# An encoder layer on one core: scores of two attention steps in one run, and feed-forward seams whose preparation is done piece by piece

## The chip, the cores and the metric

The kernel runs on one core of one Trainium2 chip. The metric is device time in microseconds (us) of one execution. PE is TensorE (matmuls), DVE is VectorE, ACT is ScalarE, POOL is GpSimd, and SP is SyncE, which here only issues DMAs. Matmul operands lie in SBUF, matmul results in PSUM, which has eight banks of 128 x 512 fp32.

## The reference

With one layer (DEPTH is 1) only the neighbourhood attention and the feed-forward are left. The same weights serve a prompt of 1024 tokens and a sample of 512 tokens, each of width 1024.

```python
h = rms_norm(x, norm_mix)
qkv = h @ w_qkv                          # 16 heads of 64
s = q . k * 64**-0.5 + bias              # each query sees a window of 8 rows x 16 columns of a grid 64 wide
o = softmax(s) @ v
x = x + o @ w_o
h = rms_norm(x, norm_ffn)
x = x + (silu(h @ w_gate) * (h @ w_up)) @ w_down      # D_FF = 2816
y = rms_norm(x, norm_final)
```

Everything is fp32.

## The kernel before

**Arithmetic.** Each fp32 operand of a matmul is split in two fp32r tiles: a "hi" copy rounded by ACT (line 138) and a "lo" rest subtracted by DVE (line 139). A product is the sum of three matmuls (hi hi, hi lo, lo hi), which is PASS. Both halves of the feed-forward use one level of a Strassen-like scheme with 7 products of 2 x 2 blocks in place of 8, so sums of blocks of the weights and of the activations must be made first, by DVE or POOL.

**Stages.** The stages follow one another on PE:

1. Norm, transposes, the V projection (lines 129, 278), then the Q and K projection of the first head pair (line 332).
2. Attention. There are 8 head pairs. A step is one column block j of a group of 512 queries and both heads of a pair: 64 steps for the prompt, 32 for the sample. A step has score matmuls `pss` (line 394), the softmax on DVE and ACT (lines 402 to 411), transposes `ptt` on PE (line 420), their split into `pT` (lines 423, 424) and the product with V, `po` (line 431). `step()` is a software pipeline: PE gets the scores of this step, the transposes of the step before, filler matmuls of the next head pair's projection (`pg`, line 332, two pieces of six), and then `po` of the step before. In the sample's steps the output projection `pgo` (line 586) is a second filler.
3. The rest of the output projection. Between its tiles, `pair()` makes the second norm of six tokens' tiles (chunk 0, the first 768 tokens), transposes them (line 668), and makes and splits the seven operands `h0` to `h6`; it does the same for chunk 1, but writes these operands to DRAM (`hop_d`, line 687). The order is: pairs of chunk 0 beside `pgo`, then the three pairs of chunk 1.
4. The feed-forward's first part: per chunk 11 units, per unit a gate and an up product (`blocks`, 7 blocks of 12 matmuls of 128 x 384, line 754). `w_ops` loads two tiles of the weight (`wr`), makes sums `wt` on DVE (lines 741 to 746) and splits into `wa` (128 x 512, six buffers) and `ws` (128 x 1024, three buffers). After chunk 0 the seven operands of chunk 1 are loaded from DRAM (`hr`) and split into the same `h` tiles. Products of a unit go to DRAM as sums (`gs`, POOL, lines 800 to 803; `gop_d`, line 805).
5. The down projection: 7 operands by 6 tiles of tokens. For each operand eleven weight tiles `wd` are split, three of the operands from differences made by POOL in `tk` (lines 848, 851, 854) and one in `dr` (line 857); for each tile one `go` (128 x 1408) is loaded and split; then 33 matmuls of 128 x 512 run (line 910). `finish()` makes the final norm and stores.

I call the borders between stages 3 and 4, between the chunks of stage 4, and between stages 4 and 5 the first, middle and third seam.

**What sets the order.** The code is written in program order for each engine, and a scheduler then orders each engine's queue by its own estimates. Every queue is executed in order, so an instruction that waits holds back all behind it on that engine. Waits come from tiles (a pool gives a tile again once its last reader is done) and from PSUM banks. PSUM tags G, S, V and T have two banks each: scores in S, transposes in T, `po` in V, projections in G.

Of the kernel before, what the change touches and what calls it, by code (L numbers as in the profile page):

```python
# [11 lines left out]
F32 = mybir.dt.float32  # L12
# [43 lines left out]
def body(tc, xp, xs, g_mix, g_ffn, g_fin, w_qkv, rpb, w_o, w_g, w_u, w_d, yp, ys):  # L56
# [9 lines left out]
    with es:  # L66
# [16 lines left out]
        hop_d = dr.tile([7, P, KB // 2, HT], F32, name="hop_d")  # L83
        gop_d = dr.tile([7, 6, P, NP, P], F32, name="gop_d")


        ident = cpool.tile([P, P + 24], F32, name="ident")[:, :P]
# [4 lines left out]
        nc.gpsimd.memset(mhalf, -0.5)  # L92

# [13 lines left out]
        def psum(tag, name, bufs=None):  # L107
            return ps.tile([P, 512], F32, tag=tag, name=name, bufs=bufs)
# [15 lines left out]
        def transpose_split(xn, hh, hl, col):  # L124
            for b in range(2):
                pt = psum("T", "pt")
# [69 lines left out]
        b_cm, bpool = pool("bpool", bufs=4)  # L196
# [33 lines left out]
        def fill_bias():  # L230
            while len(ahead) < 3:
# [183 lines left out]
        def flip(ss, n):  # L415
            out = []
            for s in ss:
                pt = psum("T", "ptt")
                for c in range(n):
                    nc.tensor.transpose(pt[:, c * P:(c + 1) * P], s[:, c * P:(c + 1) * P], ident)  # L420
                pT = ap.tile([P, 3, 2, P], F32R, tag="pT", name="pT", bufs=3)
# [25 lines left out]
        def steps(hp, g, q, k, v, n, store):  # L447
            oT = ap.tile([P, 512], F32, tag="o", name="oT", bufs=2)
            ov = oT.rearrange("p (r j i) -> p j r i", r=8, j=NJ)
            b = None  # L450
            for jj in range(2):
                pos = []
                for u in range(2):
                    j = jj * 2 + u
# [21 lines left out]
        def step(st, fillers, n):  # L476
            sc = st["s"]() if st else None
            if sc:
                next(sc)
            pT = None  # L480
# [476 lines left out]
```

## Time and profile before

| what | value |
|---|---|
| three runs | 1841.29 to 1848.37 us, median 1846.19 us |
| the profiled execution, its own time | 1845.18 us |
| its span, first to last instruction | 1843.4 us |
| PE busy | 1754.1 us, 95% of the span |
| DVE, ACT, POOL busy | 65%, 47%, 24% of the span |
| mean granted clock of PE | 0.985 |
| DMA | 278.80 MB, mean 151 GB/s |

The span and the execution's own time differ by 1.8 us, which lie around the span. "Busy" for PE includes time in which a matmul runs at a lower clock, so idle time alone does not tell what a stage loses; the count of matmuls in a stretch against its length does.

### The profile page before, as it was taken

The numbers are of one execution on the slowest core, as the hardware profiler recorded it, in microseconds if no ns is written. First come the engines' busy times: TensorE is split into PE (matmuls) and PEld (weight loads), VectorE is DVE, ScalarE is ACT, GpSimd is POOL, SyncE is SP. The second block draws the span as 40 slices with busy tenths as digits, with TensorE's granted clock in tenths as the row PEclk, the third lists the DMA queues.
The fourth block names the chain that finished last, engine by engine and source line by source line (L and its number), as shares of the span: only waits on it lengthen the run. The fifth ranks groups of instructions, "written<-read, shape, count | busy, mean of one in ns | idle before, by whom it ended". The sixth has DMA issues, their size and how long they took to land.

```text
span 1843.4 us, 25648 instructions
## 1 busy us (share of the span) xinstructions
PE 1754.1 (95%) x9178; PEld 1522.5 (83%) x9178; DVE 1192.9 (65%) x2191; ACT 863.7 (47%) x1706; POOL 448.4 (24%) x495
## 2 busy tenths in 40 slices
PE   8999999999999999979999999999999969999898
PEld 6877777777767777868999999899999958887676
DVE  4401877777896566768777777867777444545654
ACT  4411776766785554544443444444443333333322
POOL 1211000000130000112243342424243323526420
PEclk9999999999999999988999999999999979999999
DMA  7755334333464443676343434544333277635732
GB/s 245 221 183 160 111 105 113 108 101 103 126 208 146 133 149 100 221 247 185 108 121 118 133 110 151 164 129 125 108 120 107 68 272 245 225 130 191 232 129 100
DMA packets 222048, 278.80 MB, mean 151 GB/s; under 512 B 25600, under 2 KB 171776, under 8 KB 221920
## 3 DMA queue, kind: packets, MB, share of 16 engines
q1 hardware_dynamic: 201824, 210.69, 37.3%
q0 software_dynamic: 18368, 60.18, 9.5%
q10 hardware_dynamic: 1728, 6.29, 1.1%
q8 instruction: 72, 1.18, 0.3%
q14 instruction: 56, 0.46, 0.1%
HBM read 213.20 MB, written 76.43 MB: 157 GB/s over the span
## 4 chain that ended last, share of the span: by engine, by line
PE 68%; DVE 10%; DMA 9%; ACT 5%; issue 3%; SPq 2%; POOL 2%; DVEq 0%; ACTq 0%; POOLq 0%
PE pa L754 20%; PE pd L910 12%; PE pd L754 10%; PE pgv L278 7%; PE pg L332 6%; PE pb L754 5%; DMA vr<-v_d 5%; PE pgo L586 3%; DMA dr<-ffn_w_down 2%; PE pss L394 2%; PE ptt L420 2%; DVE pT L424 2%; SPq L378 2%; PE po L431 2%; ACT s L405 1%
## 5 line engine op out<-in xcount | busy, mean ns | idle before, releaser
L910 PE MATMUL pd<-wd,go 128*128 128x512 f32 x1386 | 323.0, 395 | 30.5 <-ACT go L138 20.4
L910 PEld LDWEIGHTS pd<-wd,go 128*128 128x128 f32 x1386 | 263.0, 191 | 90.4 <-ACT go L138 21.6
L754 PE MATMUL pa<-h,ws 128*128 128x384 f32 x1056 | 201.8, 339 | 2.9 <-ACT c L777 2.1
L754 PE MATMUL pa<-h,wa 128*128 128x384 f32 x1056 | 195.1, 338 | 7.0 <-ACT wa L138 4.5
L754 PE MATMUL pd<-h,ws 128*128 128x384 f32 x1056 | 198.3, 335 | 1.2 <-ACT h L138 0.6
L332 PE MATMUL pg<-hTp,whl 128*128 128x512 f32 x768 | 193.7, 399 | 0.0
L754 PEld LDWEIGHTS pa<-h,wa 128*128 128x128 f32 x1056 | 185.8, 190 | 8.9 <-ACT wa L138 5.2
L139 DVE TENSOR_TENSOR ws<-wt,ws 128x1024 fp32r<-128x1024 f32 x88 | 108.6, 1235 | 127.1 <-ACT ws L138 126.7
L754 PEld LDWEIGHTS pa<-h,ws 128*128 128x128 f32 x1056 | 185.1, 189 | 6.7 <-ACT c L777 4.3
L754 PEld LDWEIGHTS pd<-h,ws 128*128 128x128 f32 x1056 | 184.5, 188 | 1.8 <-ACT h L138 1.0
L332 PEld LDWEIGHTS pg<-hTp,whl 128*128 128x128 f32 x768 | 139.9, 188 | 27.5 <-issue 0.4
L805 POOL DMA_DIRECT2D gop_d<-c x66 | 50.5, 765 | 387.4 <-DVE c L796 380.3
L405 ACT ACTIVATE s<-s,mx 128x384 f32<-128x384 f32 (+1 forms) x192 | 110.7, 580 | 67.3 <-DVE mx L402 67.1
L586 PE MATMUL pgo<-wo,oh 128*128 128x512 f32 x576 | 139.3, 392 | 0.2 <-DVE oh L139 0.2
L139 DVE TENSOR_TENSOR wa<-wr,wa 128x512 fp32r<-128x512 f32 x132 | 117.8, 897 | 18.4 <-ACT wa L138 17.8
L138 ACT CAST ws<-wt 128x1024 fp32r<-128x1024 f32 x88 | 92.6, 1053 | 68.6 <-PE pd L754 65.4
L586 PEld LDWEIGHTS pgo<-wo,oh 128*128 128x128 f32 x576 | 105.6, 188 | 20.7 <-DVE oh L139 0.6
L138 ACT CAST go<-gr 128x1408 fp32r<-128x1408 f32 x42 | 57.7, 1374 | 131.2 <-PE pd L910 114.0
L138 ACT CAST wa<-wr 128x512 fp32r<-128x512 f32 x132 | 81.4, 621 | 62.8 <-PE pb L754 40.0
L754 PE MATMUL pb<-h,wa 128*128 128x384 f32 x528 | 102.0, 340 | 3.4 <-DVE c L774 3.4
L332 PE MATMUL pg<-hTs,whl 128*128 128x512 f32 x384 | 102.6, 404 | 0.8 <-DVE q L343 0.8
L424 DVE TENSOR_TENSOR pT<-ptt,pT 128x384 fp32r<-128x384 f32 (+1 forms) x192 | 90.0, 507 | 17.3 <-ACT pT L423 16.5
(138 smaller groups left out, 2859.6 us busy)
## 6 DMA issues: line engine op xcount, KB each, us to landing
gr<-gop_d SPq DMA_DIRECT2D x42, 704.0 KB
dr<-ffn_w_down SPq DMA_DIRECT2D x99, 256.0 KB
wr<-ffn_w_gate SPq DMA_DIRECT2D x44, 512.0 KB
wr<-ffn_w_up SPq DMA_DIRECT2D x44, 512.0 KB
wr<-na_w_qkv SPq DMA_DIRECT2D x38, 512.0 KB
gop_d<-gs POOLq DMA_DIRECT2D x88, 192.0 KB, 4.4
gop_d<-c POOLq DMA_DIRECT2D x66, 192.0 KB, 2.8
vr<-v_d SPq DMA_DIRECT2D x192, 64.0 KB
```

The costliest lines, as they stand in the source:

```text
L138: nc.scalar.copy(hi, raw)
L139: nc.vector.tensor_tensor(lo, raw, f32(hi), ALU.subtract)
L278: nc.tensor.matmul(pg, hh[a][:, k, c:c + P], wv[k // 2][b][:, k % 2], start=(k == 0 and i == 0), stop=(k == KB - 1 and i == 2))
L332: nc.tensor.matmul(pg, w[:, a, k, :], h[b][:, k, c:c + 512], start=(k == 0 and i == 0), stop=(k == KB - 1 and i == 2))
L378: nc.sync.dma_start(out=raw[:, j * P:(j + 1) * P], in_=src[:, BS[j]:BS[j] + 32, :])
L394: nc.tensor.matmul(pt[:, :n], q[h * HD:(h + 1) * HD, a, j].rearrange("p r i -> p (r i)"), kv[:, krow:krow + nrow, BS[j]:BS[j] + 32], start ...
L405: nc.scalar.activation(s[:, :n], s[:, :n], AF.Exp, bias=mx, scale=-1.0, accum_out=sm)
L424: nc.vector.tensor_tensor(pT[:, :n, 1], pv, f32(pT[:, :n, 0]), ALU.subtract)
L586: nc.tensor.matmul(pg, ohs[k // 4][:, a, k % 4], wo[:, b, k, n * 512:(n + 1) * 512], start=(k == 0 and i == 0), stop=(k == KB - 1 and i == 2))
L754: nc.tensor.matmul(bank[:, :HT], a(y, k), b[:, z, k], start=start and k == 0 and i == 0, stop=k == KB // 2 - 1 and i == 2, skip_group_chec ...
L805: nc.gpsimd.dma_start(out=gop_d[i, 3 * c:3 * c + 3, :, p].rearrange("j q t -> q j t"), in_=a.rearrange("q (j t) -> q j t", j=3))
L910: nc.tensor.matmul(pd, go[:, y, i], wds[i][:, z], start=(i == 0 and m == 0), stop=(i == NP - 1 and m == 2))
```

## The change

**Attention.** PSUM tag T is gone. S has four banks, used by scores and by transposes. A step is now a pair of column blocks: PE gets the scores of both blocks in a run of twelve matmuls, then two filler pieces, then the twelve `po` matmuls of the pair before, then the six transposes of the first block, a filler piece, the six of the second block and a filler piece. The transposes of a pair thus come in the same step as its scores, and `pT` has four buffers instead of three. The bias pool has three buffers instead of four, and two tiles are fetched ahead instead of three.

**First and middle seam.** Only the pairs of chunk 0 are prepared ahead of the feed-forward. Those of chunk 1 (`pair1`) are a generator, which `ticks` advances by a piece at every second block of chunk 0's units; `reload` of the operands of chunk 1 follows block by block in the last unit of chunk 0, into tiles one place on (`h0` to `h5` and one more, `hx`). The gain of the second norm is multiplied in after the transpose, from a tile `gT` that is loaded with gain elements across partitions as the very first DMA on SP. The last unit of chunk 0 and the first and last of chunk 1 interleave the blocks of gate and up (`LAG`). Buffers shrink: `wa` six to two (and two more for the last operand), `ws` and `wt` three to two.

**Third seam and the down projection.** `down_sums` makes the four differences of the down weights in pieces during chunk 1 (two on DVE, two on POOL for each of 11 row pairs) and stores them in DRAM (`wt_d`). The down projection then only loads and splits. `go` comes in halves (6 and 5 blocks of 128), with three `gr` loads and two splits ahead, and each weight tile is split one operand ahead, one per half tile. There are 22 `wd` tiles and 7 `dr` tiles. The squares of the final norm are taken as soon as their half is complete, and the last stores leave on two queues.

The matmuls are the same in number and shape. The order of instructions on three engines shows the three places.

PE, in the middle of the prompt's attention, before: one step (`pss` scores, `ptt` transposes, `pg` projection of the next head pair, `po` product with V).

```order
L394 MATMUL pss<-kp,q 128x384 x6
L420 MATMUL ptt<-ident,s 128x128 x6
L332 MATMUL pg<-hTp_102,whl 128x512
L332 MATMUL pg<-hTp_103,whl 128x512
L332 MATMUL pg<-hTp_102,whl 128x512 x2
L332 MATMUL pg<-hTp_103,whl 128x512
L332 MATMUL pg<-hTp_102,whl 128x512 x2
L332 MATMUL pg<-hTp_103,whl 128x512
L332 MATMUL pg<-hTp_102,whl 128x512 x2
L332 MATMUL pg<-hTp_103,whl 128x512
L332 MATMUL pg<-hTp_102,whl 128x512
L431 MATMUL po<-pT,v 128x256 x6
```

The transposes there belong to the step before, whose softmax had twelve `pg` and six `po` matmuls to finish.

PE, the same place after: a part of one step, from the end of the first filler pieces to the scores of the next pair.

```order
L335 MATMUL pg<-hTp_106,whl 128x512
L434 MATMUL po<-pT,v 128x256 x12
L423 MATMUL ptt<-ident,s 128x128 x6
L335 MATMUL pg<-hTp_106,whl 128x512
L335 MATMUL pg<-hTp_107,whl 128x512
L335 MATMUL pg<-hTp_106,whl 128x512 x2
L335 MATMUL pg<-hTp_107,whl 128x512
L335 MATMUL pg<-hTp_106,whl 128x512
L423 MATMUL ptt<-ident,s 128x128 x6
L335 MATMUL pg<-hTp_106,whl 128x512
L335 MATMUL pg<-hTp_107,whl 128x512
L335 MATMUL pg<-hTp_106,whl 128x512 x2
```

The transposes moved behind `po`, into the step of their own scores, and are split by a filler piece.

SP, at the first seam, before (`wr` weights of the feed-forward, `hop_d` operands of chunk 1 on their way to DRAM).

```order
L714 DMA wr<-ffn_w_gate 128x4x256
L687 DMA hop_d<-xt 512x1x128 x2
L714 DMA wr<-ffn_w_gate 128x4x256
L687 DMA hop_d<-tt 512x1x128 x3
L687 DMA hop_d<-xt 512x1x128
L687 DMA hop_d<-tt 512x1x128
L714 DMA wr<-ffn_w_up 128x4x256 x2
```

SP, the same place after (`xo` is the residual input of the output projection).

```order
L782 DMA wr<-ffn_w_gate 128x4x256
L589 DMA xo<-x_sample 128x512 x2
L782 DMA wr<-ffn_w_gate 128x4x256
L589 DMA xo<-x_sample 128x512 x2
L782 DMA wr<-ffn_w_gate 128x4x256
L782 DMA wr<-ffn_w_up 128x4x256 x2
L782 DMA wr<-ffn_w_gate 128x4x256
L782 DMA wr<-ffn_w_up 128x4x256 x2
```

The stores of chunk 1's operands are gone from between the weight loads. The third `wr` of the piece is the first unit's second weight tile; its place in SBUF was that of the output weights `wo`, so it waits for the last `pgo` on PE.

ACT, at the third seam, before: the last copies of the feed-forward, then all eleven weight tiles, then `go`.

```order
L772 COPY c<-pa 128x384
L777 COPY c<-pa 128x384
L780 COPY c<-pd 128x384
L138 CAST wd<-dr 128x512 x11
L138 CAST go<-gr 128x1408 x2
L914 COPY u_15096<-pd 128x512
```

ACT, the same place after.

```order
L851 COPY c<-pd 128x384
L879 ACTIVATE c<-pa 128x384
L976 DMA gff<-norm_final 128x1024
L141 CAST go<-gr 128x768
L141 CAST wd<-dr 128x512 x2
L141 CAST go<-gr 128x640
L141 CAST wd<-dr 128x512 x2
L141 CAST go<-gr 128x768
L141 CAST wd<-dr 128x512 x7
L141 CAST go<-gr 128x640
```

The first `go` half is now ahead of the weight tiles. The first of these `wd` tiles lies in the place of the operand tile `h5`, so its cast waits for the last feed-forward matmul.

The diff, cut to its core:

```diff
+        gT = cpool.tile([P, KB], F32, name="gT")
+        nc.sync.dma_start(out=gT, in_=g_ffn.rearrange("(k p) -> p k", p=P))
...
+        def psum(tag, name):
+            return ps.tile([P, 512], F32, tag=tag, name=name, bufs=4 if tag == "S" else 2)
...
+                pT = ap.tile([P, 3, 2, P], F32R, tag="pT", name="pT", bufs=4)
...
+                sc = []
+                for j in (jj * 2, jj * 2 + 1):
                     if j != 2:
                         b = next_bias()
-                    yield dict(
-                        s=lambda b=b, j=j: scores(q, k, 4 * (g == 1), 4 * n, j, lambda h: b[:, h, :n * P]),
-                        n=n, pos=pos, g=u, j=j, v=v,
-                        dst=(lambda h, jj=jj: ov[h * HD:(h + 1) * HD, jj * 2:jj * 2 + 2]) if u else None,
-                        done=(lambda: nc.gpsimd.dma_start(out=o_d[hp, :, g * 512:(g + 1) * 512], in_=oT))
-                        if j == 3 else None)
-                    fill_bias()
+                    sc.append(lambda b=b, j=j: scores(q, k, 4 * (g == 1), 4 * n, j, lambda h: b[:, h, :n * P]))
+                yield dict(s=sc, n=n, jj=jj, v=v, dst=lambda h, jj=jj: ov[h * HD:(h + 1) * HD, jj * 2:jj * 2 + 2],
...
+            sc = [x() for x in st["s"]] if st else []
+            for x in sc:
+                next(x)
+            ss = [next(x) for x in sc]
+            fill(0)
             if prev:
-                p, pss = prev.pop()
-                pT = flip(pss, p["n"])
-            ss = next(sc) if sc else None
-            run(fillers, n)
-            if pT:
-                if not p["g"]:
-                    p["pos"].extend((psum("V", "po"), psum("V", "po")))
-                weighted(pT, [x() for x in p["v"]], p["j"], p["n"], p["pos"], p["g"])
-                if p["dst"]:
-                    collect(p["pos"], p["dst"])
+                p, pT = prev.pop()
+                pos = [psum("V", "po") for _ in range(2)]
+                for u in range(2):
+                    weighted(pT[u], [x() for x in p["v"]], p["jj"] * 2 + u, p["n"], pos, u)
+                collect(pos, p["dst"])
...
+            pT = []
+            for u, x in enumerate(ss):
+                pT.append(flip(x, st["n"]))
+                fill(1 + u)
...
+            def fill(part):
+                run(fillers, 1 if part or last else 2)
...
+            nc.scalar.mul(xn, xn, rs)
...
+                nc.vector.tensor_tensor(xt[:, ks], pt.rearrange("p (k t) -> p k t", k=4),
+                                        gT[:, ks].rearrange("p (k o) -> p k o", o=1).to_broadcast([P, 4, P]),
+                                        ALU.mult)
+                yield
...
-        for j in range(3):
-            pair(1, j, to_dram(j))
...
+        r2_cm, r2p = pool("r2p", bufs=3, side="right", reuse_waits="tile")
+        a2_cm, a2p = pool("a2p", bufs=2, side="right", reuse_waits="tile")
+        hx_cm, hx = pool("hx", bufs=1, side="right", reuse_waits="tile")
...
+                b11, b12, b21, b22 = x[:, :512], x[:, 512:], y[:, :512], y[:, 512:]
+                nc.vector.tensor_tensor(b11, b12, b11, ALU.subtract)
+                yield
+                nc.vector.tensor_tensor(b12, b22, b12, ALU.subtract)
+                yield
+                nc.sync.dma_start(out=wt_d[0][i * P:(i + 1) * P, :], in_=x)
+                nc.gpsimd.tensor_tensor(b22, b22, b11, ALU.subtract)
+                yield
+                nc.gpsimd.tensor_tensor(b21, b21, b22, ALU.subtract)
+                yield
+                nc.sync.dma_start(out=wt_d[1][i * P:(i + 1) * P, :], in_=y)
...
-                fr.tile([P, 1024], F32, tag="raw2", name="wr", bufs=3)
+                r2p.tile([P, 1024], F32, tag="raw2", name="wr")
...
-                o = fr.tile([P, 2, KB // 2, P], F32R, tag="wa", name="wa", bufs=6)
+            def one(a, where=fa):
+                o = where.tile([P, 2, KB // 2, P], F32R, tag="wa", name="wa")
...
-                o = fr.tile([P, 2, 2, KB // 2, P], F32R, tag="ws", name="ws", bufs=3)
+                o = fa.tile([P, 2, 2, KB // 2, P], F32R, tag="ws", name="ws")
...
-                return fr.tile([P, 2, KB // 2, P], F32, tag="wt", name="wt", bufs=3)
+                return fa.tile([P, 2, KB // 2, P], F32, tag="wt", name="wt")
...
+            order = [0] * 7 + [1] * 7
+            if after:
+                order = [0] * LAG + [x for _ in range(7 - LAG) for x in (1, 0)] + [1] * LAG
...
+            i = ORDER[n]
+            o = h_op(n - 1) if n else h_op("x", hx)
+            for k in range(0, KB // 2, 2):
+                r = temp((2 * n + k // 2) % 4)[:, :2 * HT].rearrange("p (k t) -> p k t", k=2)
+                nc.sync.dma_start(out=r, in_=hop_d[i, :, k:k + 2])
+                hi, lo = o[:, 0, k:k + 2], o[:, 1, k:k + 2]
+                nc.scalar.copy(hi, r)
+                (nc.gpsimd if n in (2, 4) else nc.vector).tensor_tensor(lo, r, f32(hi), ALU.subtract)
...
+                if count[0] % 2 == 0:
+                    next(work, None)
...
+        pairs = (x for j in range(3) for x in pair1(j))
+        tick = ticks(pairs)
+        for p in range(NP - 1):
+            unit(0, p, hops, tick if p else idle)
+            if p == NP - 2:
+                for _ in pairs:
+                    pass
+                reload(0)
+        unit(0, NP - 1, hops, idle, lambda n: reload(n) if n < 7 else None)
+        sums = down_sums()
+        tick = ticks(sums)
...
+            unit(1, p, hops2, tick if p else idle, None if 0 < p < NP - 1 else lambda n: None)
...
-                b = keep[i]
-                nc.gpsimd.tensor_tensor(b, d_raw(i, 1, 0), b, ALU.subtract)
...
-            o = drp.tile([P, 2, 512], F32R, tag="wd", name="wd", bufs=17)
-            split(b, o[:, 0], o[:, 1])
...
-            o = dl.tile([P, 2, NP, P], F32R, tag="go", name="go", bufs=2)
-            split(r, o[:, 0], o[:, 1])
...
+        for q in range(84):
+            m, tt, h = q // 12, q % 12 // 2, q % 2
+            n = SEQ[m]
+            g_load(q + 3)
+            g_split(q + 2)
+            if q % 12 < NP:
+                d_load(m + 1, q % 12)
+            if q % 12:
+                d_split(m + 1, q % 12 - 1)
+            if not h:
+                pd = psum("GSVS"[q // 2 % 4], "pd")
+            a, b = HALF[h]
+            go = gos.pop(q)
+            for i in range(a, b):
+                for k, (y, z) in enumerate(PASS):
+                    nc.tensor.matmul(pd, go[:, y, i - a], wds[m, i][:, z], start=(i == 0 and k == 0),
...
+                add(u2[tt], pd)
+                square(u2[tt], 6 + tt, 0)
+                rs = root(6 + tt)
+                y = y_tile()
+                nc.vector.scalar_tensor_tensor(y, u2[tt], rs, gf[:, :512], ALU.mult, ALU.mult)
+                nc.sync.dma_start(out=yrow(rows(tt, 1))[:, :512], in_=y)
+                nc.scalar.mul(c22[tt], c22[tt], rs)
+                nc.scalar.dma_start(out=yrow(rows(tt, 1))[:, 512:], in_=c22[tt])
```

More of the change, by code (lines that the diff above doesn't have):

```diff
@@ L612, in body, with fill @@
             n = len(jobs[hp])
+            def fill(part):
+                run(fillers, 1 if part else 2)
+                run(ofill, 1 if part else 2)
             for i, st in enumerate(steps(hp, 2, *qk, vs, 2, None)):
[L614 to L616 removed]
+                step(st, fill)
+                for _ in range((i + 1) * n // 2 - i * n // 2):
                     chores.do()
@@ L619, in body @@
             qk = nqk
-        step(None, ofill, 2)
+        step(None, lambda part: run(ofill, 1))
         a_cm.__exit__(None, None, None)
```

396 lines of the change are left out of this document (232 added, 164 removed).

## The prediction

> **What bounds the kernel now.** I read the page first: PE is busy 95% of the span, so only what PE loses can be won, and I looked for where it loses. The windows, cut at the seams, show that (stretch in us, its length, then busy time of each engine with its count of instructions, granted clock, DMA share):
>
> ```profile
> 200.00:556.00 356.00, 339.46 (x1935) 263.53 (x1935) 288.87 (x818) 258.64 (x627) 43.93 (x66) 1.00 0.42 123
> ...
> 803.00:850.00 47.00, 33.31 (x153) 30.37 (x152) 32.48 (x49) 23.13 (x39) 3.69 (x5) 0.75 0.90 279
> 850.00:1160.00 310.00, 310.00 (x1781) 307.98 (x1780) 234.27 (x305) 135.94 (x223) 112.44 (x117) 1.00 0.41 126
> 1160.00:1170.00 10.00, 6.73 (x36) 5.84 (x35) 8.88 (x13) 4.88 (x8) 4.04 (x5) 1.00 0.90 311
> 1170.00:1480.00 310.00, 308.83 (x1773) 306.90 (x1773) 215.34 (x285) 125.05 (x206) 106.49 (x112) 1.00 0.35 107
> 1480.00:1506.00 26.00, 8.45 (x27) 6.25 (x26) 12.09 (x16) 9.40 (x13) 7.65 (x9) 0.61 0.89 315
> 1506.00:1697.00 191.00, 190.23 (x839) 157.23 (x838) 96.14 (x95) 63.53 (x80) 74.83 (x47) 1.00 0.60 203
> 1697.00:1762.00 65.00, 52.83 (x211) 40.56 (x210) 46.77 (x50) 25.42 (x44) 34.64 (x26) 0.95 0.67 223
> 1762.00:1843.40 81.40, 73.12 (x323) 60.22 (x321) 35.84 (x46) 21.32 (x37) 6.85 (x8) 0.98 0.31 109
> ```
>
> Inside the feed-forward's first part PE has no gap: 310.00 us for 1781 matmuls is 0.174 us each, which no edit here can lower. In the down projection 190.23 us for 839 is 0.227 us. With these rates the other rows give what a stage loses, half clock included. First seam: 153 x 0.174 = 26.6 us of 47.0, so at least 20.4 are lost; 48 of the 153 are transposes, which are shorter, and I take 22. Middle seam: 10.0 - 36 x 0.174 = 3.7. Down projection: 26.0 - 27 x 0.227 = 19.9 at the third seam, then 17.1 at 1697 to 1762, and 81.4 - 323 x 0.227 = 8.1 at the end: 45 in all.
>
> What PE waited for (total us, times, longest):
>
> ```profile
> PE pd L910 <- ACT go L138: 20.4, 3, 17.1
> PE po L431 <- DVE pT L424: 9.9, 14, 1.4
> PE pd L910 <- DVE go L139: 9.9, 8, 1.9
> PE pt L129 <- DVE xn L122: 8.1, 1, 8.1
> PE ptt L420 <- DVE ri L407: 5.5, 17, 1.1
> PE pa L754 <- ACT wa L138: 4.5, 1, 4.5
> PE pb L754 <- DVE c L774: 3.4, 1, 3.4
> ```
>
> The attention loses in many small waits (`po` for `pT`, `ptt` for the softmax). The timeline of PE over one undisturbed step of the prompt (start in us, its length, the matmuls):
>
> ```profile
> 187.69 0.87 PE L431 MATMUL po<-pT,v 128*128 128x256 f32 x6
> 188.49 0.80 PE L394 MATMUL pss<-kp,q 64*128 64x384 f32 x6
> 189.22 0.88 PE L420 MATMUL ptt<-ident,s 128*128 128x128 f32 x6
> 189.85 3.01 PE L332 MATMUL pg<-hTp,whl 128*128 128x512 f32 x12
> 192.70 0.87 PE L431 MATMUL po<-pT,v 128*128 128x256 f32 x6
> ```
>
> From `po` to `po` that is 192.70 - 187.69 = 5.01 us. The prompt's scores run from 179.8 to 518.2 us, where those of the sample begin:
>
> ```profile
> L394 PE MATMUL pss<-kp,q x384: 334/340/447, 179.8 to 513.7; 64*128 64x384 f32 x192
> ...
> L394 PE MATMUL pss<-ks,q x192: 276/282/387, 518.2 to 726.4; 64*128 64x256 f32 x192
> ```
>
> These 338.4 us hold 64 steps. 56 of 5.01, and 8 (the last head pair, with six `pg` instead of twelve) of 5.01 - 6 x 0.227 = 3.65, make 309.8. So 28.6 us are lost.
>
> **The change part by part.** The sum is made against the profiled execution's 1845.2 us, which lies 1.0 below the median of the runs.
>
> *Start.* `gT` is now ahead of the input on SP, and PE waits 8.1 us for that input. Its 1024 pieces of 4 bytes have no like in the trace. The nearest rows are issues on SP: a load of weights in 512 pieces, and three stores of 512 pieces each:
>
> ```profile
> 805.78 1.50 SPq L714 DMA_DIRECT2D wr<-ffn_w_gate  x1
> 807.38 3.25 SPq L687 DMA_DIRECT2D hop_d<-tt  x3
> ```
>
> A store takes 1.1 us to issue; by pieces `gT` would take twice that. A load may also be hidden in part. I take -1.5 (bounds 0 and -4).
>
> *Attention.* The transposes of a pair now come 12 `pg` and 12 `po` after its scores: by the timeline 2.85 + 2 x 0.80 = 4.4 us for two blocks' softmax. `po` follows the transposes by a filler piece, the next twelve scores and two pieces, about 5 us, where `pT` now has 3 us. Both named waits get more room. New is that a pair's second scores need a bank of S which the DVE subtraction of `pT` frees. DVE is the doubt: 288.87 us busy of 356 is 81%; the same work in 309.8 of 338.4 is 89%, and its queue is in order. I take half of the 28.6 back, 15 (bounds 4 and 26). The sample's part has fewer and shorter waits: 3 (0 to 6).
>
> *First seam.* The three pairs of chunk 1 leave it. What stays late is the second weight tile, whose place is free only after the last `pgo`. Before, a tile of this kind was issued at 805.78 + 1.50 and used at 813.59:
>
> ```profile
> 813.59 1.14 ACT L138 CAST wa<-wr 128x512 fp32r<-128x512 f32 x2 [0.17 <-DMA wr<-ffn_w_gate]
> ```
>
> That is 6.3 us with DMA at 0.90. From it go the twelve matmuls of block 0 (2.1 us); the cast adds 0.6: PE stands 4.9 us. Then block 5 needs two sums, a cast and the first subtraction:
>
> ```profile
> L138 ACT CAST ws<-wt 128x1024 fp32r<-128x1024 f32 x88 | 92.6, 1053 | 68.6 <-PE pd L754 65.4 <-issue 2.8 <-DVE wt L742 0.4
> L139 DVE TENSOR_TENSOR ws<-wt,ws 128x1024 fp32r<-128x1024 f32 x88 | 108.6, 1235 | 127.1 <-ACT ws L138 126.7
> L741 DVE TENSOR_TENSOR wt<-wr 128x512 f32<-128x512 f32 x44 | 30.1, 685 | 2.8 <-DMA wr<-ffn_w_gate 2.8
> L745 DVE TENSOR_TENSOR wt<-wr 128x512 f32<-128x512 f32 x44 | 45.8, 1041 | 0.7
> ```
>
> 2 x 0.69 + 1.05 + a part of 1.24, less the 2.1 us of block 1: another 1.5. And the clock: after a wait of 3.4 us at 844.17 the record shows
>
> ```profile
> 844.10:849.60 5.50, 5.43 (x17) 5.43 (x18) 1.24 (x2) 2.22 (x4) 0.00 (x0) 0.50 1.00 346
> 849.60:855.00 5.40, 5.40 (x32) 5.13 (x31) 4.46 (x7) 3.11 (x6) 0.00 (x0) 1.00 0.15 58
> ```
>
> 17 matmuls in 5.43 us, 2.5 more than at full rate. So the seam loses 4.9 + 1.5 + 2.6 = 9 of the 22: a gain of 13 (10 to 19; with a landing in 3 us and no halving the upper end). The Trainium skill ("TensorE: Matmul & The Clock Gate", Part 1) says that about 3.4 us without work bring half rate, and about 3.4 us of sustained work end it; that would cost 1.7 us in place of 2.5, and the seam would gain 1 more. The trace agrees on the wait, but its half rate lasts 5.4 us.
>
> *Feed-forward's buffers and added pieces.* By the queues' order a split is now possible at the earliest 73 (`wa`) and 61 (`ws`) matmuls before its use, 12.7 and 10.6 us, where it was 157 and 85; in the three interleaved units only 25 to 37, 4.3 us. A cast and a subtraction of `ws` take 2.3. DVE gets 24 pieces of 0.69 in chunk 0 (17 on 234.27 of 310) and 22 of 0.69 to 1.04 in chunk 1, where POOL gets 22 of the kind
>
> ```profile
> L851 POOL TENSOR_TENSOR tk<-dr 128x512 f32<-128x512 f32 x11 | 17.6, 1613 | 9.4 <-DMA dr<-ffn_w_down 9.4
> ```
>
> so POOL goes from 106.49 to about 142 of 310. The rows of lines 741 and 745, one operation on one size, at 685 and 1041 ns, show that DVE slows in some places; I price DVE's loss at half of POOL's added time, an estimate between nothing (line 741) and all of it: 215 + 23 + 18 = 256 of 310, 83%, still not the bound. I take -3 (0 to -12). The Trainium skill ("SBUF — State Buffer", Who interferes with whom) says that a DVE instruction with two inputs in SBUF contends with a GpSimd instruction that reads SBUF. By that rule up to all of POOL's 35 us would be lost to DVE, which would stand at 273, 88%; this term would be near its -12, and the slower rival below would get a chance of 0.15. The trace fits the rule in its direction, with 685 against 1041 ns for the same form.
>
> *Middle seam.* The reload is spread over a unit, into other tiles: of 3.7 us I take 3 (0 to 3.7).
>
> *Down projection.* At the seam, PE waited 17.1 us for `go`, behind eleven weight tiles on ACT. Now DVE's queue decides: eleven subtractions and two `go` halves, by
>
> ```profile
> L139 DVE TENSOR_TENSOR wd<-dr,wd 128x512 fp32r<-128x512 f32 x44 | 31.5, 758 | 16.0 <-ACT wd L138 15.7
> L139 DVE TENSOR_TENSOR go<-gr,go 128x1408 fp32r<-128x1408 f32 x42 | 72.6, 1727 | 44.0 <-ACT go L138 42.8
> ```
>
> 11 x 0.76 + 1.73 = 10.1 us, plus 0.6 for the last product, against 33 x 0.227 = 7.5 us of matmuls: 3 to 5 lost. The first matmul follows the last of the feed-forward after 0.6 + 0.6 + 0.8 = 2.0 us (product, cast, subtraction), no wait of 3.4; I take 5 (to 10, if the clock halves). POOL's sums, which fell due at 1697 to 1762, are gone from there, and the splits run half a tile ahead with four `go`: 3 left of 17.1 (0 to 10). The end keeps one square and one product less behind the last matmul, by
>
> ```profile
> 1836.56 0.61 ACT L884 ACTIVATE yo<-c 128x512 f32<-128x512 f32 x1
> ...
> 1838.91 0.75 DVE L892 SCALAR_TENSOR_TENSOR yo<-c,rs,gff 128x512 f32<-128x512 f32 x1
> ```
>
> 0.6 + 0.75 = 1.4: 7 left of 8. So 15 of 45 are left, a gain of 30 (20 to 37).
>
> *Sum:* -1.5 + 15 + 3 + 13 - 3 + 3 + 30 = 59.5. 1845.2 - 59.5 = 1785.7; I forecast **1785 us**.
>
> **The rivals.** (a) *The attention gains nothing*: scores wait for S banks or DVE's queue takes over at 89%. For it speaks that load; against it that the named waits each get over 1 us more room. It gives 1785 + 18 = 1803. (b) *The seams give back half*: the landing is slow again (DMA at 0.90 in both seams) and the clock halves at both. Then 21 of 43 go: 1806. (c) *Slower: the feed-forward starves.* With two `ws` tiles, ACT's cast waits for PE's last reader of the older one, and all behind it on ACT, copies of PSUM and Silu among them, waits too. If each of the 88 `ws` pairs then shows its cast (1.05) and its subtraction (1.24) behind one another, 2.3 us, the loss is 202 us at worst; if the cast alone shows, 88 x 1.05 = 92, and the time 1785 + 92 = 1877. It decides for slower from 69 / 88 = 0.8 us per pair. For it speaks that `wa` falls from six to two, and DVE's 82%; against it 10.6 us of room for 2.3 of work outside the three interleaved units. (d) *The change doesn't do what it says* (the scheduler puts pieces where they block): in the order the pieces lie where the code puts them, so this has little; it would give about 1845.
>
> **How the numbers follow.** Forecast 0.55, (a) 0.15, (b) 0.15, (c) 0.09, (d) 0.06. The bounds of the terms add up to 1845 - 92 = 1753 at best and 1845 - 18 = 1827 at worst; they won't all fall on one side, so the range goes from 1760 to 1825. It takes in (a) and (b), leaves out (c) and (d), and should hold the time 8 times in 10. 0.5% is 9 us, about what a measurement of this kernel can tell from no change. Faster by more (below 1837): forecast, (a), (b), and a remnant of (d): 0.87. Within: most of (d), 0.04. Slower: (c), 0.09.
>
> **What would show it.** Right: prompt scores that span about 323 us; at the first seam one wait of 4 to 6 us for `wr` or `wa`, no transposes; 310 us for some 1780 matmuls still between the seams; at the third seam a gap under 3.4 us and clock 1.00 after it. Wrong: PE waits named `ws`, `wa` or `c` many times in chunk 0 or 1 (then c); `pss` waiting for `pT` in every pair (then a); PEclk under 0.8 at both seams (then b).

## The result and the profile after

The changed kernel takes 1824.07 us (median of four runs, 1823.53 to 1828.39) against 1845.89: a ratio of 0.9884 (95% interval 0.986 to 0.9907), 21.8 us. The forecast was 1785. The sign was right and the time lies in the range, at its very end, but the gain, though clear of the noise, is about a third of the forecast 60 us. So the question is where some 39 us went.

The profiled execution of the changed kernel took 1828.39 us, 4.3 more than its median, so the two traces differ by 16.8 us of span only. Stage by stage they differ like this (borders are starts of the matmuls named; the middle of the feed-forward is its 1849th matmul of 3696):

| stage | before | after | gain | forecast |
|---|---|---|---|---|
| up to the first prompt score `pss` | 179.8 | 180.2 | -0.4 | -1.5 |
| prompt's attention, to the sample's first score | 338.4 | 337.0 | 1.4 | 15 |
| sample's attention, to the last `pgo` | 284.7 | 279.5 | 5.2 | 3 |
| first seam and chunk 0 | 351.3 | 355.1 | -3.8 | 13 and most of -3 |
| middle seam and chunk 1 | 327.1 | 338.2 | -11.1 | 3 and the rest of -3 |
| third seam, down projection, end | 362.1 | 336.6 | 25.5 | 30 |

A part of chunk 0's -3.8 belongs to this one execution: in six later traces whose edits leave the code of that stretch alone (e1, e4, e5, e6, e9, e12) it took 348.8 to 351.9 us.

The lines of the changed kernel behind the table, from the views of single lines of code (duration min/median/max in ns, then first and last start):

```profile
L397 PE MATMUL pss<-kp,q x384: 334/338/447, 180.2 to 510.8; 64*128 64x384 f32 x192
...
L397 PE MATMUL pss<-ks,q x192: 276/280/387, 517.2 to 715.6; 64*128 64x256 f32 x192
```

```profile
L593 PE MATMUL pgo<-wo,oh x576: 387/389/498, 561.9 to 796.7; 128*128 128x512 f32 x192
```

```profile
L822 PE MATMUL pa<-hx,wa x264: 334/337/525, 1151.8 to 1469.1; 128*128 128x384 f32 x132
```

```profile
L1066 PE MATMUL pd<-wd,go x1386: 387/392/792, 1491.1 to 1818.7; 128*128 128x512 f32 x198
```

The windows of the changed kernel, to be held against those in the prediction:

```profile
840.00:1150.00 310.00, 298.31 (x1687) 294.99 (x1686) 233.81 (x308) 136.43 (x221) 109.26 (x113) 0.97 0.49 154
...
1152.00:1270.00 118.00, 107.11 (x589) 103.92 (x588) 109.79 (x122) 41.41 (x70) 78.14 (x64) 0.98 0.85 287
1270.00:1480.00 210.00, 209.91 (x1204) 209.15 (x1203) 151.33 (x198) 84.82 (x142) 76.03 (x80) 1.00 0.37 117
...
1506.00:1780.00 274.00, 274.00 (x1179) 220.99 (x1178) 153.71 (x206) 108.87 (x181) 53.95 (x58) 1.00 0.60 193
```

Read each length with its count of matmuls. From 840 to 1150 us PE is short of 16.5 us (1687 x 0.174 = 293.5), where nothing was lost before. In the second part of chunk 1 nothing is lost, 0.174 us per matmul as before. In its first 118 us PE is short of 16 us of work (589 x 0.174 = 102.5), with DVE 93% busy. In the down projection PE is never idle, and yet a matmul takes 274 / 1179 = 232.4 ns, where it took 226.7. The waits of PE:

```profile
PE pa L822 <- ACT c L847: 10.7, 5, 4.3
PE pt L132 <- DVE xn L125: 10.3, 4, 8.7
PE pa L822 <- DVE c L854: 9.2, 8, 2.8
PE pss L397 <- DVE pT L427: 5.4, 7, 0.9
PE ptt L423 <- DVE s L412: 4.8, 5, 1.4
PE ptt L423 <- ACT s L414: 4.4, 13, 1.1
PE pb L822 <- ACT wa L141: 4.1, 1, 4.1
```

The waits of before for `go` and for `pT` at `po` are gone. New are `c` in the feed-forward (a result bank that ACT or DVE has not emptied) and `pss` for `pT`.

### The profile page after: what moved, and what is told of

Its sections match the earlier page's. It is cut to its first block, busy times and chain, and to the rows that moved or that the text cites. A ratio compares the mean times of both kernels' runs of the same rounds, so it can differ in the third digit from the quotient of the medians.

```text
span 1826.6 us, 25898 instructions
## 1 busy us (share of the span) xinstructions
PE 1755.7 (96%) x9178; PEld 1534.0 (84%) x9178; DVE 1222.2 (67%) x2263; ACT 869.9 (48%) x1742; POOL 441.4 (24%) x513
## 4 chain that ended last, share of the span: by engine, by line
PE 69%; DVE 10%; DMA 9%; ACT 4%; issue 4%; POOL 2%; SPq 2%; DVEq 0%; ACTq 0%; POOLq 0%
PE pd L1066 17%; PE pa L822 15%; PE pg L335 8%; PE pd L822 7%; PE pgv L281 6%; PE pgo L593 5%; DMA vr<-v_d 4%; PE pb L822 4%; PE pss L397 3%; PE po L434 2%; PE ptt L423 2%; SPq L381 2%; DMA t<-ffn_w_down 1%; DMA wr<-na_w_qkv 1%; ACT s L408 1%
## 5 line engine op out<-in xcount | busy, mean ns | idle before, releaser
L335 PE MATMUL pg<-hTp,whl 128*128 128x512 f32 x768 | 203.5, 409 | 0.0
L142 DVE TENSOR_TENSOR ws<-wt,ws 128x1024 fp32r<-128x1024 f32 x88 | 114.7, 1304 | 96.7 <-ACT ws L141 96.5
L822 PE MATMUL pa<-h,wa 128*128 128x384 f32 x792 | 151.5, 344 | 9.3 <-DVE c L854 9.2
L822 PEld LDWEIGHTS pa<-h,wa 128*128 128x128 f32 x792 | 141.9, 192 | 12.3 <-DVE c L854 11.7
L141 ACT CAST go<-gr 128x768 fp32r<-128x768 f32 x84 | 65.6, 782 | 150.7 <-PE pd L1066 112.4
L142 DVE TENSOR_TENSOR wa<-wr,wa 128x512 fp32r<-128x512 f32 x132 | 123.6, 948 | 11.5 <-ACT wa L141 10.4
L142 DVE TENSOR_TENSOR go<-gr,go 128x768 fp32r<-128x768 f32 x84 | 81.5, 971 | 71.6 <-ACT go L141 70.2
```

The lines of the kernel that those rows point to most:

```text
L141: nc.scalar.copy(hi, raw)
L142: nc.vector.tensor_tensor(lo, raw, f32(hi), ALU.subtract)
L335: nc.tensor.matmul(pg, w[:, a, k, :], h[b][:, k, c:c + 512], start=(k == 0 and i == 0), stop=(k == KB - 1 and i == 2))
L822: nc.tensor.matmul(bank[:, :HT], a(y, k), b[:, z, k], start=start and k == 0 and i == 0, stop=k == KB // 2 - 1 and i == 2, skip_group_chec ...
```

## Experiments

Each edit is made to the changed kernel (1824.07 us) unless another is named. Times are medians of four runs.

**e1, 128 bytes.** The wait view doesn't show why a down matmul takes 232 ns. The layout of SBUF does: the change dropped a small statistics tile (`ms2`, 128 bytes with its buffers), so all pools on the left side start 128 bytes earlier. By the addresses of the built programs, `wd` and `go` both started at 128 modulo 256 before; after, 19 of the 22 `wd` start at 0, the `go` still at 128.

```diff
-        ident = cpool.tile([P, P + 16], F32, name="ident")[:, :P]
+        ident = cpool.tile([P, P + 48], F32, name="ident")[:, :P]
```

> One tile that nothing reads grows by 128 bytes, so every pool on the left side of SBUF starts 128 bytes later; the program is otherwise the changed kernel's (1824.1 us), instruction by instruction. Theory: a matmul whose two SBUF operands start at different places modulo 256 bytes runs slower (232.4 in place of 226.8 ns for 128x512). Then the down projection's 1386 matmuls go back to about 227 ns (-7.8 us), the Q and K projection to about 230 (-2), the blocks with the last weight operand to 173 (-2), and the prompt's V projection goes from 227 to 233 (+2): about 1814. Rival: the down matmuls are slower for their half-tile waits and the splits beside them. Then nothing changes: 1824.

Measured: 1819.2 us, -4.9. The same stretch of the down projection in the changed kernel, then in e1:

```profile
1510.00:1770.00 260.00, 260.00 (x1119) 209.65 (x1118) 148.24 (x198) 104.02 (x175) 52.12 (x54) 1.00 0.61 194
```

```profile
1510.00:1770.00 260.00, 260.00 (x1148) 215.36 (x1148) 149.78 (x202) 106.00 (x177) 50.62 (x52) 1.00 0.61 195
```

1119 matmuls against 1148 in 260 us: 232.3 against 226.5 ns, with the same instructions in the same order. The theory's 7.8 us for this stage are met: first to last down matmul 320.0 us against 327.6. The whole is not: by medians e1 gains 4.9 us, about half of the 10 forecast. The spans of the two traces differ by 9.4 us (1817.2 and 1826.6), but 6.3 of that is chunk 0, where the changed kernel's trace was slow by itself. The Q and K projection hardly followed: the median of its 768 prompt matmuls stayed at 393 ns, though its two operands start alike in e1 and did not in the changed kernel. The prompt's V projection went the forecast way (first score at 181.3 us in place of 180.2). Its lines before, after, and in e1 (weights at 0, 128 and 0, activations at 128 in all three):

```profile
L278 PE MATMUL pgv<-wv,hTp x384: 388/393/795, 9.9 to 134.6; 128*128 128x512 f32 x192
```

```profile
L281 PE MATMUL pgv<-wv,hTp x384: 387/389/796, 10.5 to 134.6; 128*128 128x512 f32 x192
```

```profile
L281 PE MATMUL pgv<-wv,hTp x384: 390/393/796, 10.6 to 136.1; 128*128 128x512 f32 x192
```

So in these two stages it counts whether the two operands of a matmul lie alike. In all their fast cases both are at 128, so a start at 0 could be what is slow; the feed-forward speaks against that. In the changed kernel `h0`, `h1` and `wa` of the `pb` blocks all start at 0, and such a matmul of 128x384 lasts 334 ns in the median (line 822), while the blocks with `hx`, at 128, and `wa`, at 0, last 337, and 334 in e1, where both are at 128. Why the Q and K projection does not follow is open. The rival of half-tile waits falls for the down projection.

**e2, the first weight.** Of the raw weight tiles two in five lie in a pool that is free early; a start of the count one lower gives the first unit both of them.

```diff
-        turn = [0]
+        turn = [-1]
```

> The first unit's second weight tile is given a place that is free early, instead of one that the output weights hold until the last pgo. Theory: at the first seam PE waits 4.1 us for this tile, and the halved clock after it costs some 3 more; both go, and the time is 1817 (1815 to 1820). Rival: the wait is the transfer's own, in a stretch of busy DMA, and the next tile is late in its place: 1822 to 1825.

Measured: 1817.64, -6.4, as the theory had it. The timeline of PE at the seam, changed kernel, then e2:

```profile
796.93 2.27 PE L822 MATMUL pa<-h,wa 128*128 128x384 f32 x12
803.33 1.01 PE L822 MATMUL pb<-h,wa 128*128 128x384 f32 x2 [4.12 <-ACT wa L141]
```

```profile
796.19 2.27 PE L822 MATMUL pa<-h,wa 128*128 128x384 f32 x12
798.30 2.24 PE L822 MATMUL pb<-h,wa 128*128 128x384 f32 x12
```

The wait and the slow matmuls behind it (two in 1.01 us) are gone; the longest wait of PE in e2 from 790 to 840 us is 1.3.

**e3, the scaling that waited for POOL.** The timeline of the changed kernel, where PE waits longest in chunk 0 (lines of DVE and the weight loads left out):

```profile
900.03 0.77 POOL L894 DMA_DIRECT2D gop_d<-c  x1
...
900.79 3.05 POOL L894 DMA_DIRECT2D gop_d<-gs  x4
...
903.86 0.57 POOL L681 TENSOR_TENSOR rs<-me,mhalf 128x1 f32<-128x1 f32 x1
904.47 1.15 ACT L683 ACTIVATE t<-t,rs 128x1024 f32<-128x1024 f32 x1 [2.81 <-POOL rs L681]
905.52 0.46 ACT L847 COPY c<-pa 128x384 f32<-128x384 f32 x1
...
906.03 1.33 PE L822 MATMUL pa<-h,ws 128*128 128x384 f32 x3 [3.71 <-ACT c L847]
```

A power of 128 numbers stands on POOL behind a unit's sums and stores. ACT's scaling waits for it, the copy of a finished bank waits behind the scaling, and PE waits for the bank.

```diff
             yield
+            yield
+            yield
             nc.scalar.mul(xn, xn, rs)
...
-        tick = ticks(pairs)
+        tick = ticks(pairs, True)
```

Here `True` holds the first instruction of each piece on ACT, DVE and POOL behind the last one that the code wrote before it on that engine.

> In chunk 0 the scaling of a token tile on ACT comes two pieces later than the power on POOL that it needs, and the pieces are held to their place in the code on ACT, DVE and POOL. Theory: the power stands behind POOL's sums and stores of the unit, ACT waits for it, and PSUM copies behind it hold PE twice for 3.7 and 4.3 us, each followed by 5 us of halved clock: without that 1811 (1808 to 1815), and no wait of PE for c of line 847 above 1 us in chunk 0. Rival: chunk 0 loses because two wa and two ws buffers are too few; the waits then move to other places: 1820 to 1826.

Measured: 1814.12, -10.0 (1811.21 to 1822.67). The trace is that of the run of 1822.67. PE's waits from 840 to 1140 us of e3:

```profile
PE pa L824 <- ACT c L849: 5.2, 4, 2.6
PE pa L824 <- ACT c L842: 0.5, 1, 0.5
PE pa L824 <- DVE ws L142: 0.3, 1, 0.3
```

Against 8.0 us in two waits up to 4.3 in the changed kernel; the wait of 2.6 is above the 1 that the theory allowed, so a part stays. ACT's two waits for the power in the changed kernel's chunk 0, 5.6 us, are gone. The stretch of first seam and chunk 0 took 345.9 us, 9 less than in the changed kernel's trace but only 3 to 6 less than in the six others. So the mechanism is shown, and the size of 10.0 rests on runs that spread over 11 us. PE hardly waits for `wa` and `ws`, the buffers that I had doubted; no run gives them more tiles, so what they cost elsewhere is not shown.

**e4, the sums spread.** In the order that the scheduler made, all eleven pairs of rows lie in the first four units of chunk 1 (line 768 starts first at 1163.8 us, last at 1263.4), though the code spreads them over eight. The changed kernel's timeline of DVE in one of them:

```profile
1228.02 0.68 DVE L142 TENSOR_TENSOR wa<-wr,wa 128x512 fp32r<-128x512 f32 x1
...
1229.69 1.76 DVE L142 TENSOR_TENSOR wa<-wr,wa 128x512 fp32r<-128x512 f32 x1
1231.38 1.81 DVE L768 TENSOR_TENSOR t<-t,t 128x512 f32<-128x512 f32 x1
1233.12 2.31 DVE L142 TENSOR_TENSOR ws<-wt,ws 128x1024 fp32r<-128x1024 f32 x1
```

```diff
-        tick = ticks(sums)
+        tick = ticks(sums, True)
```

> The down weights' differences are held to their place in the code, so that they spread over eight units of chunk 1 instead of bunching in the first four. Theory: in those four units DVE is 94% busy and PE loses about 2 us per unit and 5 at the start; spread out, the loss falls from 13 us to 3: 1814 (1812 to 1818). Rival: the differences cost PE the same wherever they lie, through contention of POOL and DVE: 1822 to 1826.

Measured: 1814.92, -9.1, as the theory had it. Chunk 1 took 330.2 us in place of 338.2. In e4 line 768 is spread:

```profile
L768 DVE TENSOR_TENSOR t<-t,t x11: 678/683/684, 1188.6 to 1402.9; 128x512 f32<-128x512 f32 x11
```

DVE works as long in chunk 1 as in the changed kernel, 265 us, at another density:

```profile
1145.00:1262.00 117.00, 115.38 (x655) 114.74 (x655) 97.21 (x121) 47.50 (x80) 57.69 (x52) 0.99 0.60 201
1262.00:1475.00 213.00, 209.42 (x1194) 207.29 (x1194) 167.88 (x206) 82.84 (x137) 98.27 (x93) 1.00 0.51 173
```

The median of line 768 fell too, from 1.50 to 0.68 us. So whether the gain comes from the density alone, or also from which operations run beside POOL's, is not told apart.

**e5, the attention as before.** The whole attention part of the diff is undone.

```diff
-            return ps.tile([P, 512], F32, tag=tag, name=name, bufs=4 if tag == "S" else 2)
+            return ps.tile([P, 512], F32, tag=tag, name=name, bufs=2)
...
-                    step(st, fill)
+                    step(st, fillers, 1 if last else 2)
```

> The changed kernel with the attention as it was before (single steps, scores and transposes in two banks each); all the rest as changed. Theory: the pairs are worth what the two traces show, 1.4 us in the prompt and 5.2 in the sample's part, so undoing them gives 1831 (1828 to 1834), with prompt scores over 338 us. Rival: they are worth the forecast 18 us and something else took it back: 1840 or more.

Measured: 1829.28, +5.2. So the pairs are worth about 5 us, near the traces' 6.6, not 18. Nearly all of it lies in the sample's part (284.5 us in place of 279.5); the prompt took 337.9, just short of the 338 that the theory asked, in place of 337.0.

**e6, rests on POOL.**

```diff
-            split(rv, vv[:, :, 0:4:3, :], vv[:, :, 1:3, :])
+            nc.scalar.copy(vv[:, :, 0:4:3, :], rv)
+            nc.gpsimd.tensor_tensor(vv[:, :, 1:3, :], rv, f32(vv[:, :, 0:4:3, :]), ALU.subtract)
```

and likewise for the unscaled `whl`.

> In the attention the low rests of the V tiles and of the unscaled weight tiles are subtracted on POOL, which is idle there, instead of DVE: some 41 us less for DVE within the prompt's scores (289 of 337 us busy before). Theory: the pairs' scores wait for a bank that DVE's subtraction of pT frees late, because DVE's queue is nearly full; with room there the prompt's scores take 327 us or less in place of 337, and the time is 1812 (1808 to 1817). Rival: the order of PE itself, with its chain of scores, softmax and transposes, sets the pace: prompt 334 or more, time 1820 to 1825.

Measured: 1819.77, -4.3, between the two. Its prompt scores:

```profile
L403 PE MATMUL pss<-kp,q x384: 334/338/448, 181.1 to 504.4; 64*128 64x384 f32 x192
L403 PE MATMUL pss<-ks,q x192: 276/279/578, 511.3 to 711.3; 64*128 64x256 f32 x192
```

511.3 - 181.1 = 330.2 us in place of 337.0. So the subtractions on DVE are a part of the cause, not all. The link that the theory named is not shown: PE's wait for `pT` at `pss` did not fall, it was 5.4 us and is now 7.0.

**e7, the reload without POOL.**

```diff
-                (nc.gpsimd if n in (2, 4) else nc.vector).tensor_tensor(lo, r, f32(hi), ALU.subtract)
+                nc.vector.tensor_tensor(lo, r, f32(hi), ALU.subtract)
```

> All the subtractions of the reloaded operands are on DVE; before, four of fourteen were on POOL. Theory: the two on POOL at the end of chunk 0 (2.0 us each) hold up two-input subtractions on DVE (2.4 in place of 0.7, 2.9 in place of 1.2), which make PE wait 2.9 us and halve its clock: 1819 (1817 to 1821). Rival: DVE is simply full there; with 3.6 us more it is worse: 1824 to 1828.

Measured: 1819.51, -4.6, as the theory had it. At the end of chunk 0, changed kernel:

```profile
1141.50 4.08 POOL L908 TENSOR_TENSOR h<-t,h 128x768 fp32r<-128x768 f32 x2 [5.13 <-ACT h L907]
1141.54 2.36 DVE L814 TENSOR_TENSOR wt<-wr,wt 128x512 f32<-128x512 f32 x1
...
1147.79 4.21 PE L822 MATMUL pa<-h,wa 128*128 128x384 f32 x12 [2.75 <-DVE c L854]
```

In e7 the same operation of line 814 takes 0.7 us there, and PE has no gap from 1128 to 1142 us:

```profile
1128.00:1142.00 14.00, 14.00 (x82) 14.00 (x81) 13.82 (x20) 10.50 (x16) 0.76 (x1) 1.00 0.77 248
```

That is 82 matmuls in the last 14 us before chunk 1, where the changed kernel got 50 through (1138 to 1152). DVE is 99% busy there too, with 20 instructions in 14 us, and PE is fed: here contention counted, not load. The Trainium skill ("SBUF — State Buffer", Who interferes with whom), by which a DVE instruction with two inputs in SBUF contends with a GpSimd instruction that reads SBUF, agrees with these rows: 2.36 us beside POOL, 0.68 without.

**e8, four together.** The edits of e1 to e4.

> The four edits e1 to e4 together. They gave -4.9, -6.4, -10.0 and -9.1 us each for itself. Theory: they remove separate losses and add up: 1794 (1790 to 1799). Rival: the losses share a cause, DVE's load, and come back elsewhere: 1802 to 1812.

Measured: 1801.8 (1794.48 to 1803.52), -22.3, at the edge of the rival's 1802. By medians three quarters of the single gains add up. By the traces the stages add: first seam and chunk 0 take 344.9 us in e2, 345.9 in e3 and 341.1 in e8, against 348.8 to 351.9 without either; chunk 1 takes 330.2 in e4 and 329.3 in e8, the last stage 328.7 in e1 and 328.8 in e8. So most of the missing 8 us is probably e3's 10.0, of which its trace shows 3 to 6; the rival's shared cause is not needed for it. PE still waits nine times, 9.1 us in all, for ACT's copies of line 849. In the longest of them (2.1 us, at 1087.16) ACT had stood 4.7 us for a result of DVE (`c` of line 845), not for a `ws` tile.

**e9, side jobs apart.** `step` of a pair was followed by two side jobs; now one comes after the scores' fillers.

```diff
             def fill(part):
                 run(fillers, 1 if part or last else 2)
+                if part == 0:
+                    chore()
...
-                    for _ in range(2):
-                        if i in (0, 1, 2, 5, 6, 7) or last:
-                            chores.do()
-                        i += 1
+                    chore()
```

> The changed kernel does the side jobs of two steps (loading and splitting V and weight tiles) back to back at the end of a pair; here one comes after the scores' first fillers and one at the end, all else as changed. Theory: two casts of V in a row make ACT wait for the second one's load (13.3 us in ten waits in the prompt), which holds the softmax's scaling and the split of pT behind it: apart, the prompt's scores take 332 us or less in place of 337, the time is 1819 or less. Rival: ACT's waits move with the jobs, as before the change, where they were 20.5 us: 335 to 339 us and 1822 to 1826.

Measured: 1825.79, prompt 339.4: no gain, as the rival had it. ACT's wait for V even rose from 13.3 to 26.7 us.

**e10, six together.** e8, e6, e7 and a spare tile in the pool of the V weights.

```diff
         with tc.tile_pool(name="vpool", bufs=2) as vp:
+            vp.tile([P, 32], F32, name="vpad", bufs=1)
```

> The four edits of e8 (1801.8 us) with the rests on POOL (e6, -4.3), the reload's subtractions on DVE (e7, -4.6) and a spare tile of 128 bytes ahead of the V projection's weights, so that these too lie with their partner modulo 256 (576 matmuls x 5.6 ns, -3.2). Theory: most of it adds: 1790 (1786 to 1795). Rival: as between e1 to e4 and e8, a quarter or more is lost: 1794 to 1800.

Measured: 1787.77 (1783.53 to 1790.16), a ratio to the kernel before of 0.9682 (0.9661 to 0.9703). It is within the theory's range and beats both kernels: 36.3 us less than the changed one.

**e11, e10 with the side jobs of e9.**

> e10 with the side jobs apart as in e9. Theory: with less work on DVE and with the jobs apart, the prompt's scores reach 325 us or less and the time is 1785 (1780 to 1790). Rival: both cure the same wait, and it is as e10 within 2 us.

Measured: 1798.54, 10.8 worse than e10; neither theory. The loss lies in the attention: the prompt's scores take 337.7 us in place of 332.8, the sample's part 288.4 in place of 281.8.

**e12, one load of four.** On e6:

```diff
-            for j in range(NJ):
+            for j in range(1):
                 nc.sync.dma_start(out=raw[:, j * P:(j + 1) * P], in_=src[:, BS[j]:BS[j] + 32, :])
...
-            rv = raw[:, :512].rearrange("p (j h d) -> p j h d", j=NJ, h=2)
+            rv = raw[:, :P].rearrange("p (j h d) -> p j h d", j=1, h=2).to_broadcast([P, NJ, 2, HD])
```

> e6 (1819.8 us) with one of the four loads of a V tile; its block stands for all four column blocks, so three quarters of V's columns are left out, with casts and subtractions of the same size as before. Theory: what e6 still loses in the prompt (330 us against 310 of matmuls) comes from ACT's wait for these loads, which SP issues one after the other in 2.3 us, ahead of the split of pT: the prompt's scores take 325 us or less, ACT's wait for the loads falls from 11.7 us in the prompt to 4 or less, and the time is 1814 or less. Rival: ACT waits for the place of the tile, not for the transfer, or the loss is elsewhere: 329 or more, 1818 to 1822.

Measured: 1806.35, 13.4 less than e6, the largest single effect, most of it in the sample's attention (269.5 us in place of 281.1). Its scores, and PE's waits from 181 to 508 us:

```profile
L403 PE MATMUL pss<-kp,q x384: 334/338/445, 180.7 to 499.8; 64*128 64x384 f32 x192
L403 PE MATMUL pss<-ks,q x192: 276/280/387, 506.7 to 695.1; 64*128 64x256 f32 x192
```

```profile
PE ptt L429 <- ACT s L420: 5.5, 8, 0.8
...
PE pss L403 <- DVE pT L433: 0.3, 1, 0.3
```

The prompt takes 326.0 us, close to the 325 of the theory, and the wait of `pss` for `pT` falls from 7.0 to 0.3 us. But the link that the theory named fails: ACT's wait for the loads is not 4 us or less, but 18.7. So the loads of V are shown to cost the attention some 4 us in the prompt and 12 in the sample; whether by SP's time to issue four of them, by their landing, or by what they hold up, is open.

## Why the prediction was wrong, step by step

By the table, 27.9 us are missing in the two stages of the feed-forward (13 forecast, -14.9 measured), 11.4 in the attention (18 and 6.6) and 4.5 in the last stage; the start was 1.1 better.

**Start.** -0.4 for -1.5, by luck. The V projection got faster here because its operands came to lie alike. In e1, where they lie as before, the first score starts at 181.3 us, 1.5 later than before: the term was right, and hidden.

**Attention, the first step that failed.** "Both named waits get more room" was half wrong. PE's waits from the prompt's first score to the sample's, before, then in the changed kernel:

```profile
PE po L431 <- DVE pT L424: 5.5, 6, 1.3
PE ptt L420 <- DVE ri L407: 3.0, 13, 0.4
PE ptt L420 <- ACT s L411: 2.4, 7, 0.4
```

```profile
PE pss L397 <- DVE pT L427: 5.4, 7, 0.9
PE ptt L423 <- ACT s L414: 3.8, 12, 1.1
PE ptt L423 <- DVE s L412: 1.0, 2, 0.8
```

`po` no longer waits for `pT`, but `ptt` waits for the softmax almost as long as before, 4.8 us for 5.4. And the new wait, `pss` for the bank that `pT` frees, which I named and priced at nothing of its own, came with the size of the one that went, as rival (a) said. So of 15 us in the prompt 1.4 came, and e5 puts the pairs at 5.2 us in all. e6 and e12 show two things that held the prompt back: the subtractions on DVE (6.8 us) and the loads of V (4.2 more). The prediction weighed the first as a doubt and left the second out.

**First seam.** Right in kind and size: the wait was 4.1 us where I had 4.9, followed by a halved clock, and e2 prices it at 6.4 us. From 797 to 840 us 207 matmuls took 43 us, so 7 are lost where I had 9. The second wait, for the sums, did not come.

**The feed-forward's added pieces, the step that failed most.** The term was -3 (0 to -12); the trace loses 16.5 us from 840 to 1150 us and 15.5 from 1152 to 1270. I judged the pieces by DVE's total load (83% forecast for chunk 1; it was 265 of 338 us, 78%) and by the room for splits. The load was about right and did not tell the cost. Three orders cost 23.7 us by medians: ACT behind POOL's queue (e3, 10.0), the sums bunched (e4, 9.1), POOL's rests beside DVE's in the reload (e7, 4.6). "In the order the pieces lie where the code puts them", with which I dismissed rival (d), was wrong: the eleven pairs of rows lay in four units instead of eight. Rival (c) had the right place, PE's waits for `c` in the feed-forward, but for the waits that e3, e4 and e7 removed not the mechanism, too few `ws`.

**Middle seam.** Not 3 us back: the reload put POOL's subtractions beside DVE's (e7, counted above), and the bunched sums followed on it. In e7 PE has no gap there.

**Down projection.** 25.5 of 30, right in kind: no wait of 17 us, and PE's first matmul follows the last of the feed-forward after 1.1 us (1491.1 and 1490.0), not 2.0, though the clock did fall (0.89 from 1490 to 1506 us). The missing part is no wait at all: 7.6 us of slower matmuls, a cost that the prediction left out by taking the rate of 0.227 us as fixed. In e1, without it, this stage gains 33.4.

The costs found, 4.9 + 6.4 + 10.0 + 9.1 + 4.6 + 4.3, make 39 one by one. e10 has all of them and the spare tile for V (3.2 expected), and gains 36.3. Its 1788 us is near the forecast, but not by the forecast's sum: against the kernel before, the attention gains 8.6 of the 18 and the last stage 33.6 where 30 was forecast. Why e11 is slower than e10 is not explained.

## What to carry to other kernels

When work is spread into the gaps of a full pipeline, its busy time says little: for each piece ask which in-order queue it stands in, what it waits for there, and who stands behind it, and read from the order where the scheduler really put it. Even a tiny operation on a slow queue (a power of 128 numbers behind POOL's stores) can hold three engines. And compare the time per matmul, busy time over count, before looking for waits: a rate that changed by 2.5% over 1386 matmuls cost 7.6 us here, more than the wait of 4.1 us at the first seam, which every view of waits shows.

## What the runs showed of the hardware

A 128x512 matmul took 232 to 233 ns from start to start where its two SBUF operands started at different places modulo 256 bytes (0 and 128), and 227 where both started at 128: the down projection before, after and in e1, the V projection before, after and in e1. The Q and K projection does not show it, and no other distance was tried.

The clock can halve after a shorter wait than I had taken: after 2.75 us without a matmul, at 1147.79 in the rows of e7's comparison, twelve matmuls took 4.21 us in place of 2.1. The wait's length alone does not decide it. At the same place in e1:

```profile
1148.05 2.35 PE L822 MATMUL pa<-h,wa 128*128 128x384 f32 x12 [2.74 <-DVE c L854]
```

The Trainium skill ("TensorE: Matmul & The Clock Gate", Part 1) gives about 3.4 us without work for this; the trace agrees for waits of 3.7 and 4.1 us, and at 2.75 us it differs.
